# Padded small tiles, 512-column weight blocks, gate products among the decay's, and one inversion after the other in a two-layer decoder trunk

## The chip, the cores and the metric

The kernel runs on one core of one Trainium2 chip, in one launch. The metric is the device time of that launch in microseconds. A run differs from another of the same kernel by a few microseconds (2192.98 to 2197.68 here). The engines are named as in the profile: PE is TensorE (PEld its weight loads), DVE is VectorE, ACT is ScalarE, POOL is GpSimd, SP is SyncE, which issues most DMAs.

## What is computed

Two layers over 512 positions and 1024 features, in float32. Layer 0 is a half-step SwiGLU feed-forward (FFN), an RWKV-7 time mix and another half-step FFN. Its output gives one shared set of keys and values. Layer 1 is a half-step FFN, differential attention on the shared keys and values, and a last half-step FFN. Cut to what the change touches:

```python
def swiglu(h, w_in, w_out):                      # w_in 1024 x 5632, w_out 2816 x 1024
    gate, up = jnp.split(h @ w_in, 2, axis=-1)
    return (jax.nn.silu(gate) * up) @ w_out

def rwkv7_time_mix(h, mu, w_rkv, w0, w1, w2, a0, a1, a2, g1, g2, ...):
    dx = h_prev - h
    r, k, v = jnp.einsum('sbtc,scd->sbtd', h[None] + dx[None] * mu[:3, None, None, :], w_rkv)
    w_log = -jax.nn.softplus(-(w0 + jnp.tanh(xw @ w1) @ w2)) - 0.5
    decay = jnp.exp(-jnp.exp(w_log.astype(jnp.float32)))
    a = jax.nn.sigmoid(a0 + (xa @ a1) @ a2)
    g = jax.nn.sigmoid(xg @ g1) @ g2
    ...
    y = wkv7_scan(heads(r), heads(decay), heads(k), heads(v), -kk, kk * a_h)
    ...
    return (y.astype(h.dtype) * g) @ w_o

def shared_kv(x, kv_norm, w_kv, k_norm):
    kv = rms_norm(x, kv_norm) @ w_kv             # first half keys, second half values
```

## The kernel before

Activations lie with features on the 128 partitions and the 512 positions along the free axis: eight tiles `x` of 128 x 512. Every product in float32 is made of three fp32r matmuls: weight and activation are each split into a high and a low half (`whi`, `wlo`, `xgh`, `xgl`, `acth`, `actl`), and `mm3` (lines 196 to 198) adds high x high, high x low and low x high in one PSUM bank. A raw weight block `wraw` comes by DMA on SP, ACT copies it to `whi`, and DVE subtracts to `wlo`. In a row of the trace the moving operand stands first, the stationary one second.

The work goes in this order. **FFN** (four times, `ffn`): 22 pairs of gate and up features in three groups of 8, 8 and 6; in-products move `xgh` and `xgl` over `whi` and `wlo` (512 columns); out-products (`out`) move `acth` and `actl`, 12 buffers in the FFN's own pool. In the last FFN the last group is `natural`: there the act tiles are stationary, weights are moved in blocks of 256 columns (`wblock_k`, 4 rows of k to a tile), for each block the four position tiles t follow one another, and each result of 128 x 256 is added and stored at once. **Time mix** (`rwkv`): LoRA products (weights in BK, then sA), then for p of 0 to 7 a decay and an a product of 64 rows, each followed by a sigmoid on ACT (lines 650 and 652); `mixed(2)` makes the values' input (`xmt` scaled on ACT, line 636, added on DVE, line 637, then split, `xgl` on line 204); then eight gate products of four matmuls, copied by ACT to the single buffer `t0` (line 669) and stored to g_d; then `values`, four blocks of 256 columns, into four PSUM banks a block, while `recs` makes the decay's scans on DVE (line 680, tile `t1`); then the keys, where `key_done` also makes the `scores` that the inversion needs, then the receptances r. The inversion solves two groups of triangular blocks by 31 dependent steps of two DVE instructions each (lines 815 and 816): `inv0` works on x2 and x3 with the scratch tile `nr_t`, `inv1` on x0 and x1 with `nr_a`. From the seventh key on the program writes steps of `inv0` and then, by `both`, one step of each in turn. After it the results go through DRAM boxes, and the scan (`wkv`) begins with the products of line 952. **Shared KV**: keys by `heads`, values in four blocks of 256 columns, t by t, with `vN` scaled on ACT. **Attention** and the last FFN follow.

The order of the instructions on each engine isn't the order of the text: the tile framework schedules them at build time, by its own timeline and by when buffers come free. Addresses are set at build time too. `Rn` (line 279) is a tile of 4 numbers a partition in the pool `gp`, and `gk` (`trunk`, line 1366) of one in `kvp`, and pools lie one above the other. In the built program `xgh`, `xgl`, `whi`, `wlo`, `wraw` and `x` start 416 bytes past a multiple of 512 in each partition; BK, the act, g and u tiles of the first, second and last FFN, and kT and vN start at 448; act, g and u of the third FFN, which runs while `kvp` is open, start at 480.

## Time and profile before

| | |
|---|---|
| median of 3 runs | 2196.48 us (2192.98 to 2197.68) |
| the profiled execution | 2192.3 us, its span 2190.6 us |
| granted PE clock, mean of the span | 0.988 of full |
| PE busy | 2129.4 us, 97% of the span |
| DVE, ACT, POOL busy | 1193.8, 834.3 and 220.8 us (54%, 38%, 10%) |
| first, second, third, last FFN | some 16 to 375, 812 to 1198, 1296 to 1656, 1798 to 2187 us |
| time mix | some 375 to 812 us |

A row of the timeline gives an instruction's start and its length. Matmuls are pipelined, so the next begins before the last one's length is over: the distance of two starts is what one costs PE in a stream, and the length is more. A wait's row names the waiting instruction, what released it, and how long the engine stood. The granted clock is a share of full speed, where 1.00 is 2.4 GHz and 0.50 is 1.2.

### The profile page before, as it was taken

How to read it: one execution, taken by the hardware profiler on the slowest of the kernel's cores; microseconds unless marked ns; L12 is line 12 of the kernel's file. 1: busy time of each engine (PE TensorE's matmuls, PEld its weight loads, DVE VectorE, ACT ScalarE, POOL GpSimd, SP SyncE). 2: the span in 40 equal slices, each digit the busy share in tenths (PEclk: the TensorE clock that was granted, in tenths of full speed). 3: DMA queues.
4: the chain of work that ended last, by engine and by line, in shares of the span. 5: the costliest groups of instructions: out<-in, count | busy, mean ns of one | idle time of the engine just before them, and what ended most of it. 6: DMA issues, size and time to landing. Idle time of an engine off the chain costs nothing.

```text
span 2190.6 us, 27632 instructions
## 1 busy us (share of the span) xinstructions
PE 2129.4 (97%) x11007; PEld 1801.0 (82%) x11007; DVE 1193.8 (54%) x1902; ACT 834.3 (38%) x1429; POOL 220.8 (10%) x259
## 2 busy tenths in 40 slices
PE   9999999899969999999999999999999999999999
PEld 7888888687769878888888998888889678888888
DVE  6445445588847865444445535445356855444443
ACT  5223223688225544222224443222235754222222
POOL 1101000000232310100000001001010111100000
PEclk9999999999979999999999999999999999999999
DMA  7622333245587633322223232222332112222222
GB/s 264 221 93 87 115 101 119 64 141 140 125 195 188 174 113 96 96 96 96 96 91 101 78 97 96 96 96 96 96 96 78 40 39 96 97 95 96 96 92 82
DMA packets 276636, 239.90 MB, mean 110 GB/s; under 512 B 57114, under 2 KB 269244, under 8 KB 276508
## 3 DMA queue, kind: packets, MB, share of 16 engines
q1 hardware_dynamic: 275740, 236.05, 34.5%
q0 software_dynamic: 768, 2.10, 0.6%
q8 instruction: 86, 1.41, 0.3%
q14 instruction: 42, 0.34, 0.1%
HBM read 202.98 MB, written 28.84 MB: 106 GB/s over the span
## 4 chain that ended last, share of the span: by engine, by line
PE 87%; DVE 6%; ACT 3%; DMA 2%; issue 1%; POOL 0%; SPq 0%; DVEq 0%; ACTq 0%
PE ps L196 27%; PE ps L197 27%; PE ps L198 27%; DVE s L1190 1%; PE ps L994 1%; PE ps L958 1%; DMA g_d<-t 1%; PE ps L970 0%; PE ps L1189 0%; PE ps L993 0%; PE ps L952 0%; PE ps L964 0%; DMA am_d<-nsq 0%; DMA wraw<-in_rwkv_w_rkv_dram 0%; PE ps L985 0%
## 5 line engine op out<-in xcount | busy, mean ns | idle before, releaser
L196 PE MATMUL ps<-xgh,whi 128*128 128x512 f32 x1688 | 658.9, 393 | 4.0 <-ACT BK L652 1.9
L197 PE MATMUL ps<-xgl,whi 128*128 128x512 f32 x1688 | 657.5, 391 | 0.0
L198 PE MATMUL ps<-xgh,wlo 128*128 128x512 f32 x1688 | 649.8, 390 | 0.0
L161 ACT CAST whi<-wraw 128x1024 fp32r<-128x1024 f32 (+2 forms) x296 | 303.2, 1028 | 883.3 <-PE ps L197 582.9
L162 DVE TENSOR_TENSOR wlo<-wraw,whi 128x1024 fp32r<-128x1024 f32 (+2 forms) x296 | 426.7, 1445 | 93.0 <-ACT whi L161 83.9
L196 PEld LDWEIGHTS ps<-xgh,whi 128*128 128x128 f32 x1688 | 316.9, 188 | 74.6 <-ACT BK L652 3.0
L197 PEld LDWEIGHTS ps<-xgl,whi 128*128 128x128 f32 x1688 | 317.7, 188 | 66.5 <-issue 1.4
L198 PEld LDWEIGHTS ps<-xgh,wlo 128*128 128x128 f32 x1688 | 317.6, 188 | 65.8
L395 POOL TENSOR_TENSOR u<-u,g 128x512 f32<-128x512 f32 x88 | 124.3, 1413 | 1382.2 <-ACT whi L161 882.2
L196 PE MATMUL ps<-acth,whi 128*128 128x512 f32 x656 | 258.5, 395 | 0.0
L198 PE MATMUL ps<-acth,wlo 128*128 128x512 f32 x656 | 258.1, 394 | 0.0
L197 PE MATMUL ps<-actl,whi 128*128 128x512 f32 x656 | 258.0, 393 | 0.0
L394 DVE TENSOR_TENSOR u<-ps,R 128x512 f32<-128x512 f32 x88 | 60.8, 691 | 288.9 <-PE ps L198 288.9
L437 DVE SCALAR_TENSOR_TENSOR x<-ps,x 128x512 f32<-128x512 f32 x88 | 60.5, 690 | 224.1 <-PE ps L198 224.0
L196 PE MATMUL ps<-whi,xgh 128*128 128x256 f32 x512 | 145.6, 289 | 3.7 <-ACT t L669 3.5
L198 PEld LDWEIGHTS ps<-acth,wlo 128*128 128x128 f32 x656 | 123.0, 188 | 29.8
L197 PEld LDWEIGHTS ps<-actl,whi 128*128 128x128 f32 x656 | 123.0, 187 | 29.2
L197 PE MATMUL ps<-wlo,xgh 128*128 128x256 f32 x512 | 145.1, 285 | 1.8 <-DVE wlo L178 1.8
L196 PEld LDWEIGHTS ps<-acth,whi 128*128 128x128 f32 x656 | 123.1, 188 | 28.6
L198 PE MATMUL ps<-whi,xgl 128*128 128x256 f32 x512 | 144.4, 284 | 0.0
L391 DVE TENSOR_TENSOR g<-ps,R 128x512 f32<-128x512 f32 x88 | 60.8, 691 | 107.8 <-PE ps L198 107.7
L203 ACT CAST acth<-u 128x512 fp32r<-128x512 f32 x88 | 54.7, 621 | 123.9 <-POOL u L395 123.9
(330 smaller groups left out, 2404.0 us busy)
## 6 DMA issues: line engine op xcount, KB each, us to landing
wraw<-in_ffn_w_in_dram SPq DMA_DIRECT2D x87, 1024.0 KB, 5.1
wraw<-in_ffn_w_out_dram SPq DMA_DIRECT2D x32, 1024.0 KB, 5.0
boxes<-nr_a SPq DMA_DIRECT2D x64, 192.0 KB, 3.9
wraw<-in_ffn_w_out_dram SPq DMA_DIRECT2D x16, 768.0 KB, 4.3
wraw<-in_rwkv_w_rkv_dram SPq DMA_DIRECT2D x12, 1024.0 KB, 5.4
wraw<-in_w_kv_dram SPq DMA_DIRECT2D x8, 1024.0 KB, 5.3
am_d<-nsq SPq DMA_DIRECT2D x16, 256.0 KB
AM<-am_d SPq DMA_DIRECT2D x16, 256.0 KB, 4.3
```

What stands on the lines that cost most here:

```text
L161: self.nc.scalar.copy(hi[:, ks], raw[:, :, c : c + P])
L162: (eng or self.nc.vector).tensor_sub(lo[:, ks], raw[:, :, c : c + P], hi[:, ks].bitcast(F32))
L196: mm(ps, wh, xh, start=start, stop=False)
L197: mm(ps, wh, xl, start=False, stop=False)
L198: mm(ps, wl, xh, start=False, stop=stop)
L203: self.nc.scalar.copy(hi, src)
L391: nc.vector.tensor_mul(g, pg, self.R)
L394: nc.vector.tensor_mul(u, pu, self.R)
L395: nc.gpsimd.tensor_mul(u, u, g)
L437: nc.vector.scalar_tensor_tensor(x, ps, 0.5, x, ALU.mult, ALU.add)
L958: mm(p1[:, p, :], bbd[:, p, :], mv[:, p, :], start=True, stop=True)
L994: mm(py[:, p, cols], V[:, p, :], KM[:, p, cols], start=c == 0, stop=True)
```

## The change

There are four parts.

1. `Rn` becomes a tile of 128 numbers a partition of which four are used, `gk` one of 128 of which one is used. In the built program after it, every tile named above with 448 or 480 starts at 416.
2. A new generator `wrows` gives weights row by row: raw tiles of 4 rows of k x 512 columns, high and low tiles of 2 x 512. The values of the time mix, the values of the shared KV and `natural` take two blocks of 512 columns instead of four of 256. In the first block of `natural` and in both value products, k is the outer loop and t the inner one, over four PSUM banks; in `natural`'s second block t is the outer loop. Each output goes out in eight pieces of 128 x 512 rather than sixteen of 128 x 256.
3. The gate product q stands after decay product q + 3, its weights are loaded ahead of the loop, and its copy is DVE's, to `t1` with two buffers. `mixed(2)` comes after the loop, and its scaling is DVE's.
4. `both` goes. `feed` runs six steps of `inv0` at k of 2, 4 and 6, and `inv1` is run from `r_done` and after it.

```diff
+    def wrows(self, src):
+        nc = self.nc
+        kt = src.shape[0] // P
+        src = src.rearrange("(k p) f -> p k f", p=P)
+        for k in range(0, kt, 2):
+            if k % 4 == 0:
+                n = min(4, kt - k)
+                raw = self.tl(self.wp, "wraw", (P, 4, 512), bufs=2)
+                nc.sync.dma_start(raw[:, :n], src[:, k : k + n, :])
+            r = raw[:, k % 4 : k % 4 + 2]
+            hi = self.tl(self.wp, "whi", (P, 2, 512), F32R, bufs=3)
+            lo = self.tl(self.wp, "wlo", (P, 2, 512), F32R, bufs=3)
+            nc.scalar.copy(hi, r)
+            nc.vector.tensor_sub(lo, r, hi.bitcast(F32))
+            for i in range(2):
+                yield hi[:, i], lo[:, i]
...
-        rn = self.tl(self.gp, "Rn", (P, 4))
+        rn = self.tl(self.gp, "Rn", (P, P))[:, 0:4]
...
-                for b in range(0, C, 256):
-                    wb = self.wblock_k(w_out[j0 * P : j1 * P, b : b + 256])
+                for b in range(0, C, 512):
+                    wb = self.wrows(w_out[j0 * P : j1 * P, b : b + 512])
...
-                    t = self.tl(kt, "xmt", bufs=2)
-                    nc.scalar.activation(t, h[k][:, 1:], AF.Copy, scale=self.omu[:, i : i + 1])
+                    if s == 2:
+                        nc.vector.tensor_scalar_mul(t, h[k][:, 1:], self.omu[:, i : i + 1])
+                    else:
+                        nc.scalar.activation(t, h[k][:, 1:], AF.Copy, scale=self.omu[:, i : i + 1])
...
-                t = self.tl(kt, "t0")
-                nc.scalar.copy(t, ps)
-                nc.sync.dma_start(d["g"][p], t)
+            for p in range(KT + 3):
+                if p < KT:
...
+                if p >= 3:
+                    q = p - 3
+                    c = slice(q * P, (q + 1) * P)
+                    ps = self.ps()
+                    self.mm3(ps, g2h[:, c], g2l[:, c], gh, gl, True, False)
+                    mm(ps, w3[:, c], z3, start=False, stop=True)
+                    t = self.tl(kt, "t1", bufs=2)
+                    nc.vector.tensor_copy(t, ps)
+                    nc.sync.dma_start(d["g"][q], t)
+            xv = mixed(2)
...
-            def values(blocks, x, vn_of, aside):
-                for b in blocks:
-                    wb = self.wblock_k(prm["w_rkv"][2][:, b * 256 : (b + 1) * 256])
-                    pss = [self.ps()[:, :256] for _ in range(4)]
+            def values(x, vn_of, aside):
+                for b in range(2):
+                    wb = self.wrows(prm["w_rkv"][2][:, b * 512 : (b + 1) * 512])
+                    pss = [self.ps() for _ in range(4)]
+                    for k, (hi, lo) in enumerate(wb):
+                        for t in range(4):
+                            tt = slice(t * P, (t + 1) * P)
+                            self.mm3(pss[t], x[k][0][:, tt], x[k][1][:, tt], hi, lo, k == 0, k == KT - 1)
...
-            def both():
-                for _ in range(40):
-                    run(inv0, 1)
-                    yield
-                    run(inv1, 1)
-                    yield
...
+                if k in (2, 4, 6):
+                    run(inv0, 6)
...
-                run(steps, 10)
+                run(inv1, 5)
...
-            run(steps, 80)
+            run(inv1, 40)
...
-        gk = kvp.tile([P, 1], F32, tag="gk", name="gk")
+        gk = kvp.tile([P, P], F32, tag="gk", name="gk")[:, 0:1]
```

How this stands in the built order, at three places. The first is PE where the decay's products end and the gate's begin. Before (`xgh_2831` is the input of the decay and a products, `xgh_2866` that of the gate's; L667 is the gate's fourth matmul):

```order
L196 MATMUL ps_2989<-xgh_2831,whi_2910 128x512
L197 MATMUL ps_2989<-xgl_2832,whi_2910 128x512
L198 MATMUL ps_2989<-xgh_2831,wlo_2911 128x512
L196 MATMUL ps_3064<-xgh_2866,whi_3052 128x512
L197 MATMUL ps_3064<-xgl_2867,whi_3052 128x512
L198 MATMUL ps_3064<-xgh_2866,wlo_3053 128x512
L667 MATMUL ps_3064<-xgh_2900,whi_3056 128x512
L196 MATMUL ps_3072<-xgh_2866,whi_3052 128x512
L197 MATMUL ps_3072<-xgl_2867,whi_3052 128x512
```

After (L702 is that fourth matmul now):

```order
L702 MATMUL ps_2968<-xgh_2900,whi_2920 128x512
L702 MATMUL ps_2986<-xgh_2900,whi_2920 128x512
L215 MATMUL ps_2999<-xgh_2831,whi_2910 128x512
L216 MATMUL ps_2999<-xgl_2832,whi_2910 128x512
L217 MATMUL ps_2999<-xgh_2831,wlo_2911 128x512
L215 MATMUL ps_3004<-xgh_2866,whi_2916 128x512
L216 MATMUL ps_3004<-xgl_2867,whi_2916 128x512
L217 MATMUL ps_3004<-xgh_2866,wlo_2917 128x512
L702 MATMUL ps_3004<-xgh_2900,whi_2920 128x512
L215 MATMUL ps_3012<-xgh_2831,whi_2910 128x512
L216 MATMUL ps_3012<-xgl_2832,whi_2910 128x512
```

The eight gate products stood in a row behind the last decay product; now the first gate products stand among the decay's, and all eight still come before the first value product.

The second place is DVE in the same stretch. Before (L178 makes the values' `wlo`, L637 and L204 the values' input):

```order
L637 SCALAR_TENSOR_TENSOR xmt_3008<-h_396_2644,vec_534,xmt_3008 128x512
L637 SCALAR_TENSOR_TENSOR xmt_3015<-h_397_2645,vec_534,xmt_3015 128x512
L178 TENSOR_TENSOR wlo_3138<-wraw_3135,whi_3137 128x1024
L204 TENSOR_TENSOR xgl_3012<-xmt_3008,xgh_3011 128x512
L204 TENSOR_TENSOR xgl_3019<-xmt_3015,xgh_3018 128x512
L178 TENSOR_TENSOR wlo_3142<-wraw_3135,whi_3141 128x1024
L178 TENSOR_TENSOR wlo_3294<-wraw_3291,whi_3293 128x1024
L637 SCALAR_TENSOR_TENSOR xmt_3022<-h_398_2646,vec_534,xmt_3022 128x512
L637 SCALAR_TENSOR_TENSOR xmt_3029<-h_399_2647,vec_534,xmt_3029 128x512
```

After (L704 copies a gate product to `t1`, L667 scales the values' input, L670 and L223 are the old L637 and L204, L197 the old L178):

```order
L704 COPY t_477_3009<-ps_3004 128x512
L223 TENSOR_TENSOR xgl_3090<-xmt_3086,xgh_3089 128x512
L704 COPY t_481_3027<-ps_3022 128x512
L667 TENSOR_SCALAR xmt_3100<-h_398_2646,omu 128x512
L223 TENSOR_TENSOR xgl_3097<-xmt_3093,xgh_3096 128x512
L670 SCALAR_TENSOR_TENSOR xmt_3100<-h_398_2646,vec_534,xmt_3100 128x512
L667 TENSOR_SCALAR xmt_3107<-h_399_2647,omu 128x512
L704 COPY t_485_3045<-ps_3040 128x512
L197 TENSOR_TENSOR wlo_3142<-wraw_3139,whi_3141 128x1024
L704 COPY t_487_3053<-ps_3048 128x512
```

The gate's copies and the scalings are now DVE's, between the pieces of the values' input, and four of the copies stand ahead of the values' first `wlo`; the fifth is right ahead of it.

The third place is DVE in the inversion, during the r products. Before (x2, x3 and nr_t are `inv0`'s, x0, x1 and nr_a are `inv1`'s):

```order
L815 TENSOR_TENSOR nr_t_682_4218<-x2_520_3133,x3_521_3134 128x256
L815 TENSOR_TENSOR nr_a_754_4600<-x0_518_3131,x1_519_3132 128x60
L816 TENSOR_TENSOR x3_521_3134<-x3_521_3134,nr_t_682_4218 128x16x16
L816 TENSOR_TENSOR x1_519_3132<-x1_519_3132,nr_a_754_4600 128x30x2
L815 TENSOR_TENSOR nr_t_682_4218<-x2_520_3133,x3_521_3134 128x255
L815 TENSOR_TENSOR nr_a_754_4600<-x0_518_3131,x1_519_3132 128x87
```

After (L841 and L842 are the old L815 and L816):

```order
L841 TENSOR_TENSOR nr_t_674_4006<-x2_520_3133,x3_521_3134 128x256
L841 TENSOR_TENSOR nr_a_746_4427<-x0_518_3131,x1_519_3132 128x60
L842 TENSOR_TENSOR x3_521_3134<-x3_521_3134,nr_t_674_4006 128x16x16
L842 TENSOR_TENSOR x1_519_3132<-x1_519_3132,nr_a_746_4427 128x30x2
L841 TENSOR_TENSOR nr_t_674_4006<-x2_520_3133,x3_521_3134 128x255
L841 TENSOR_TENSOR nr_a_746_4427<-x0_518_3131,x1_519_3132 128x87
```

Nothing moved here: the same steps of both groups alternate at the same place, as they do from `inv1`'s first step to `inv0`'s last, and POOL's instructions keep their order in the whole program.

## Rows read from the trace of the kernel before

**Rows 1.** The page, parts 1 and 4: busy time, and the chain that ended last.
```profile
PE 2129.4 (97%) x11007; PEld 1801.0 (82%) x11007; DVE 1193.8 (54%) x1902; ACT 834.3 (38%) x1429; POOL 220.8 (10%) x259
...
PE 87%; DVE 6%; ACT 3%; DMA 2%; issue 1%; POOL 0%; SPq 0%; DVEq 0%; ACTq 0%
```

**Rows 2.** Waits of TensorE, all: us in total, times, longest.
```profile
PE ps L952 <- DMA x<-boxes: 19.6, 1, 19.6
...
PE ps L196 <- ACT t L669: 3.5, 2, 2.2
...
PE ps L196 <- ACT BK L652: 1.9, 1, 1.9
PE ps L197 <- DVE wlo L178: 1.8, 1, 1.8
```

**Rows 3.** Timeline, TensorE: start us, us, line; first and last products of runs.
```profile
121.69 0.40 PE L196 MATMUL ps<-acth,whi 128*128 128x512 f32 x1
...
166.50 0.40 PE L196 MATMUL ps<-xgh,whi 128*128 128x512 f32 x1
...
253.35 0.39 PE L198 MATMUL ps<-xgh,wlo 128*128 128x512 f32 x1
...
375.54 0.40 PE L196 MATMUL ps<-xgh,BK 128*128 128x512 f32 x1
...
386.26 0.40 PE L197 MATMUL ps<-xgl,BK 128*128 128x512 f32 x1
...
1404.49 0.40 PE L196 MATMUL ps<-acth,whi 128*128 128x512 f32 x1
...
1448.23 0.39 PE L198 MATMUL ps<-acth,wlo 128*128 128x512 f32 x1
```

**Rows 4.** The page, part 5: count, busy us, mean ns of one, idle before.
```profile
L196 PE MATMUL ps<-acth,whi 128*128 128x512 f32 x656 | 258.5, 395 | 0.0
```

**Rows 5.** Timeline, TensorE: products of 256 columns, shared KV and last block.
```profile
1214.71 0.28 PE L196 MATMUL ps<-whi,xgh 128*128 128x256 f32 x1
...
1215.91 0.28 PE L197 MATMUL ps<-wlo,xgh 128*128 128x256 f32 x1
...
2152.89 0.37 PE L196 MATMUL ps<-whi,acth 128*128 128x256 f32 x1
...
2186.93 0.28 PE L198 MATMUL ps<-whi,actl 128*128 128x256 f32 x1
```

**Rows 6.** Instructions by line and form, VectorE: count, busy us, mean ns.
```profile
L437 DVE SCALAR_TENSOR_TENSOR x<-ps,x 128x512 f32<-128x512 f32 x88 | 60.5, 690 | 224.1 <-PE ps L198 224.0
...
L1234 DVE COPY qT<-ps 128x512 f32<-128x512 f32 x8 | 5.5, 684 | 2.1 <-ACT qsq L1230 2.1
...
L1177 DVE TENSOR_SCALAR bias<-toe 128x512 f32<-128x512 f32 x8 | 3.2, 413 | 0.0
```

**Rows 7.** DMA issues: count, KB each, median us from issue to landing.
```profile
x_d<-x SPq DMA_DIRECT2D x8, 256.0 KB, 2.1
...
out_dram<-xn SPq DMA_DIRECT2D x16, 128.0 KB, 1.7
```

**Rows 8.** Timeline, TensorE: first decay product and first key product.
```profile
404.42 0.96 PE L196 MATMUL ps<-xgh,whi 64*128 64x512 f32 x5
...
478.80 0.40 PE L196 MATMUL ps<-xgh,whi 128*128 128x512 f32 x1
```

**Rows 9.** Stretches: busy us and count per engine, granted clock, DMA share, GB/s.
```profile
404.00:490.00 86.00, 78.52 (x515) 70.51 (x513) 65.01 (x87) 69.95 (x132) 0.00 (x0) 0.94 0.34 111
410.00:420.00 10.00, 8.07 (x25) 5.73 (x23) 3.51 (x6) 9.96 (x18) 0.00 (x0) 0.66 0.00 0
440.00:450.00 10.00, 10.00 (x86) 10.00 (x85) 8.84 (x12) 10.00 (x26) 0.00 (x0) 1.00 0.36 111
```

**Rows 10.** The chain of waits, 386 to 520 us: start us, us, what.
```profile
427.63 5.21 DMA g_d<-t
```

**Rows 11.** Timeline, VectorE: a step of the second group's inversion.
```profile
601.44 0.43 DVE L816 TENSOR_TENSOR x<-x,nr_a 128x255 f32<-128x255 f32 x1
```

More of the change, by code (lines that the diff above doesn't have):

```diff
@@ L635, in mixed @@
                     t = self.tl(kt, "xmt", bufs=2)
[L636 removed]
+                    if s == 2:
+                        nc.vector.tensor_scalar_mul(t, h[k][:, 1:], self.omu[:, i : i + 1])
+                    else:
+                        nc.scalar.activation(t, h[k][:, 1:], AF.Copy, scale=self.omu[:, i : i + 1])
                     nc.vector.scalar_tensor_tensor(t, h[k][:, 0:T], self.v("mu", i), t, ALU.mult, ALU.add)
@@ L643, in rwkv @@
             wh, wl = self.wflat([(prm["w2"], 0), (prm["a2"], 64)], P)
[L644 to L655 removed]
+            g2h, g2l = self.wflat([(prm["g2"][0:P], 0)], P)
             w3 = self.tl(self.wp, "whi", (P, 8, P), F32R, bufs=3).rearrange("p k f -> p (k f)")[:96]
@@ L662, in rwkv @@
             self.tl(self.wp, "wlo", (P, 8, P), F32R, bufs=3)
-            for p in range(KT):
-                c = slice(p * P, (p + 1) * P)
-                ps = self.ps()
-                self.mm3(ps, wh[:, c], wl[:, c], gh, gl, True, False)
-                mm(ps, w3[:, c], z3, start=False, stop=True)
-                t = self.tl(kt, "t0")
-                nc.scalar.copy(t, ps)
-                nc.sync.dma_start(d["g"][p], t)
+            for p in range(KT + 3):
+                if p < KT:
+                    c = slice(p * P, (p + 1) * P)
+                    for i, hh in enumerate(half):
+                        ps = self.ps()
+                        self.mm3(ps, wh[hh, c], wl[hh, c], zh[hh], zl[hh], True, True)
+                        if i == 0:
+                            nc.scalar.activation(A[:, p, :], ps, AF.Sigmoid, bias=self.v("w0", p))
+                        else:
+                            sig = nc.scalar.activation(BK[:, p, :, 0:L], ch(ps), AF.Sigmoid, bias=self.v("a0", p))
+                if p >= 3:
+                    q = p - 3
+                    c = slice(q * P, (q + 1) * P)
+                    ps = self.ps()
+                    self.mm3(ps, g2h[:, c], g2l[:, c], gh, gl, True, False)
[4 more added lines that the diff above has]
+            xv = mixed(2)
+            xvl = self.last.ins
             oka = self.tl(kt, "oka", (P, KT))
@@ L734, in recs @@
                     yield
-            xq = lambda i: X[i].rearrange("p a (t f) -> p a t f", f=256)
-            values(range(4), xv, lambda b: [xq(2 + b % 2)[:, i] for i in range(2)], recs())
+            values(xv, lambda b: X[2 * b : 2 * b + 2], recs())
             def key_cb(p, ps):
@@ L844, in rwkv @@
             xr = mixed(0)
-            def both():
-                for _ in range(40):
-                    run(inv0, 1)
-                    yield
-                    run(inv1, 1)
-                    yield
-            steps = both()
             def feed(k):
```

76 lines of the change are left out of this document (30 added, 46 removed).

## The prediction, as it was made

> **What bounds the kernel now.** I read the page's busy shares and its chain first: TensorE (PE) is busy 97% of the span and 87% of the chain that ended last is PE [rows 1]. So time is won in two ways only: fewer or shorter matmuls, and the few places where PE waits. For the first I took the distance from one matmul's start to the next, not the durations: durations overlap (0.39 us each, a new one every 0.23), starts don't. For the second I read PE's waits: one of 19.6 us in front of the scan, and 3.5, 1.9 and 1.8 us in the stretch from 404 to 490 us [rows 2], where the change moves most. That stretch I then read by tenths and by engine.
>
> **Part 1, the padded tiles.** `Rn` takes 16 bytes and `gk` 4 before, 512 each after. In the built program the tiles allocated above `Rn` start 448 bytes past a multiple of 512 (the act tiles of the first, second and last FFN, and BK), those above `gk` 480 (the third FFN's), while xgh, whi and wlo start at 416. After, all start at 416. In-products move xgh over whi, both at 416: 384 starts from 166.50 to 253.35 us, 86.85/383 = 226.8 ns [rows 3]. Out-products have the same shape and differ by the moving tile, act: at 448, 192 from 121.69 us to the next product's start at 166.50 44.81/192 = 233.4 ns; at 480, 192 from 1404.49 to 1448.23 us, 43.74/191 = 229.0 ns [rows 3]. The LoRA products, with BK at 448 as the weight and xgh moving, go from 375.54 to 386.26 us in 46 steps of 233.0 ns [rows 3]. Two unrelated tiles at 448 cost 6.4 ns a matmul and one at 480 costs 2.2, all at the full clock, so I read this as a price of the tiles' starts. Of the 656 x 3 out-products [rows 4] 528 are in each of the first three FFNs and 384 in the last: 1440 x 6.5 + 528 x 2.2 = 10.5 us, and some 120 LoRA products x 6 ns = 0.7. They run back to back on PE, so all of it is on the path: **-11.2 us**. Bounds: 0 if the offset isn't the cause, 11.2.
>
> The Trainium skill ("SBUF — State Buffer", section "Operand start alignment") asks only that an operand start at a multiple of its element size, and "TensorE: Matmul & The Clock Gate" ("Step-by-step: what each phase is for") gives PE two independent read ports, one for the streamed operand and one for the weights. By these a start of 448 is as good as 416, and this part would give nothing. The rows at 226.8, 229.0 and 233.4 ns speak against it, but no row shows one product at two starts.
>
> **Part 2, blocks of 512 instead of 256.** One product of 512 moving columns takes the place of two of 256: by the count of rows in the order that is 192 pairs in the values of the time mix, 192 in those of the shared KV and 144 in the last FFN's final block, 528 PE rows fewer. 256-column products start every 120 ns (1214.71 to 1215.91 us in ten steps) and those of the last block every 118.6 (2152.89 to 2186.93 us, 287 steps) [rows 5]. Two of them are 240 or 237, one wide one 226.8: 13 and 10 ns a pair. Shared KV 192 x 13 = 2.5 us, last block 144 x 10 = 1.5: **-4.0 us**; the values' 2.5 are counted in part 3. Weights come in chunks of 2 x 512 instead of 4 x 256, so ACT and VectorE (DVE) convert as much, and PE works 24 x 0.227 = 5.4 us on each: no new wait. Below it can't go, since the count is fixed; above, 4.0 is all.
>
> "TensorE: Matmul & The Clock Gate" in the Trainium skill (section "Back-to-back issue gap") gives N/2.4 + 2.5 ns for a warm product alone, 215.8 for 512 columns and 109.2 for 256; merging would then save 2.5 ns a pair, some 1.3 us with the values in place of 6.5. The rows, 120 and 226.8, decide for the larger.
>
> The tail gets longer: DVE's last addition goes from 128x256 to 128x512, which takes 0.69 us in the other FFNs, about 0.3 more, and the last output is 256 KB, for which x_d's row says 2.1 us where 128 KB take 1.7 [rows 6, 7]: **+0.7 us** (0.3 to 1).
>
> **Part 3, the stretch from 404 to 490 us.** Before, the decay and a products start at 404.42 us and the first key product at 478.80 [rows 8]: 74.4 us. PE's work there is 48 decay, 32 gate and 384 value products: 80 x 0.230 + 384 x 0.120 = 64.5, so 9.9 are lost: PE outruns the sigmoids on ACT (1.9 us on BK), and the gap costs it the clock too (0.66 granted from 410 to 420), then it waits on the gate's PSUM banks (3.5 us on t, because ACT's copy waits for g_d's landing to free the single t buffer, 5.2 us the longest in the chain), and 1.8 on wlo [rows 2, 9, 10]. After, the order has the gate's products between the decay's, ahead of any value product, so PE has 32 products to do while ACT's 16 sigmoids go by; the copies are on DVE, with two buffers; the values are 192 x 0.227 = 43.6. PE needs 80 x 0.227 + 43.6 = 61.8 us: the most to be won is 12.6.
>
> What is late next is DVE. Between 404 and 490 it is busy 65.0 of 86 us [rows 9]. It gets 8 copies from PSUM (0.684 by the nearest row) and 8 multiplications (0.413) [rows 6]: 8.8 us by durations, and since such rows overlap where one follows another, while the busy time counts no overlap, I take 7.7. Then 72.7 us of DVE work, in order, must be done before the first keys' last steps; with some 3 to 4 us at the start in which it has nothing, that is 76 to 77 us from 404 where it took 86: the keys' first results come about **9.5 us** earlier. I take that, with the range 0 (all of DVE's 21 idle us stay) to 12.6. ACT loses the 8 copies and 8 of its scalings, and isn't late.
>
> What waits behind the new DVE copies: each needs its PE product and a t1 buffer, which is free when g_d two copies ago has landed; behind the fifth stands the first wlo of the values, behind the eighth the decay scans, which take t1 too. With two buffers and landings up to 5.2 us [rows 10] a copy can go every 2.9 us at worst, 23 us for eight, and PE has value products from the fifth on. SP issues the values' second raw block ahead of the last two g_d; it needs only the conversion of the first.
>
> **Part 4, the inversion.** The text changes (inv0 alone at k = 2, 4, 6, then inv1), but DVE's rows of lines 815 and 816 stand in the same order in both programs, two and two alternating, and so do GpSimd's rows: the scheduler sets it. The wait of 19.6 us for boxes, which the inversion's end is behind [rows 2], stays: **0**, bounds 0 and -9 (below).
>
> **Sum.** 11.2 + 4.0 + 9.5 - 0.7 = 24.0 us off the profiled run's 2192.3 (span 2190.6): 2168.3. The median of the three runs, 2196.48, lies 4.2 above that run, so **2172** by the median.
>
> **Rivals.** (1) The starts don't matter and out-products are slower for something else, such as the engines that write act while PE reads it: part 1 falls away, 24.0 - 11.2 = 12.8, 2183 by the median. For it: no row with one product at both starts. Against: 448 gives the same price to act and to BK, 480 another. (2) DVE bounds the middle: its idle 21 us can't be used since they are waits for h, the scores and ACT, and the 7.7 us come on top: part 3 gives 0, 2182 by the median. For it: DVE at 8.8 of 10 from 440 to 450 [rows 9]. Against: those tenths are the backlog of what ACT's late copies held up. (3) The inversion does run alone. The steps of inv1 stand between inv0's, up to 0.43 us each [rows 11] and some 33 of them until inv0's end; at 0.28 from start to start they take 9 us, and the wait shrinks by that: 2163. Against: the order. (4) **Slower**: DVE's in-order waits for g_d. If landings with two 1 MB weight blocks under way take far longer than the 5.2 us seen, copies pace everything behind them. It decides once it eats the whole 24.0 us. The seven steps between eight copies, 2.9 us each at the pace above, must then take 24/7 = 3.4 us more, 6.3; two buffers make that 12.6 a landing and its copy, so landings of 12 us, over twice the longest row [rows 10]. From there it is 2197 and up; at 16 us the steps are 8.3, 38 us are lost, and it is 2211.
>
> **How the numbers follow.** Forecast 0.66, (1) 0.12, (2) 0.13, (3) 0.04, (4) 0.05. Range: the forecast's own is 2165 to 2177 (part 3 between 5 and 12.6, the tail); up to the rivals (1) and (2) it reaches 2185; below, 2163. (3) and (4) and both of (1) and (2) together stay out. This kernel can be told from no change at about 0.2%, 4.4 us. All of the forecast, (1), (2) and (3) are faster by more; with (1) and (2) together (0.02) it would be near the bound: faster 0.93, same 0.03, slower 0.04.
>
> **What would show it.** Right: out-products and LoRA products at 227 ns in all four FFNs; 512-column products at 227 in the values, the shared KV and the last block; the first key product about 64 to 66 us after the first decay product, without waits on L669's copy; the 19.6 us wait unchanged. Wrong: out-products still at 233 (rival 1); PE waits on wlo or xgl in the values, DVE without idle time from 404 on and the first keys not earlier (rival 2); a shorter wait before L952 (rival 3); DVE idle on g_d landings (rival 4).

## The result: 2168.9 us, where the 24.4 us came from

The changed kernel took 2168.89 us (median of four runs, 2167.57 to 2170.8) against 2196.78 for the kernel before on the same chip; the ratio is 0.9877, 95% interval 0.986 to 0.9894. Its profiled execution took 2167.88 us with a span of 2166.2, so the two spans differ by 24.4 us; by the medians it is 27.9, and 21.7 and 24.2 in two later sets of runs of the same program. The prediction was 24.0 off the profiled run, 2172 by the median, with 2163 to 2185 as its range. The profiled runs differ as the sum said; the median of the changed kernel lies only 1.0 us above its profiled run, and not 4.2 as in the kernel before, which is where 2172 is too high.

The page of the changed kernel, its parts 1 and 5; they answer to [rows 1, 4]:

```profile
PE 2111.3 (97%) x10479; PEld 1772.6 (82%) x10479; DVE 1199.1 (55%) x1908; ACT 822.9 (38%) x1395; POOL 221.3 (10%) x259
...
L215 PE MATMUL ps<-acth,whi 128*128 128x512 f32 x656 | 254.7, 389 | 0.0
```

PE is 18 us less busy and still 97% of its span. The out-products' mean length falls from 395 to 389 ns, which says little; the starts say it. The timeline of PE in the changed kernel, the same runs of products as in [rows 3, 8]:

```profile
121.85 0.39 PE L215 MATMUL ps<-acth,whi 128*128 128x512 f32 x1
...
165.37 0.39 PE L215 MATMUL ps<-xgh,whi 128*128 128x512 f32 x1
...
372.09 0.39 PE L215 MATMUL ps<-xgh,BK 128*128 128x512 f32 x1
...
382.74 0.40 PE L217 MATMUL ps<-xgh,BK 128*128 128x512 f32 x1
...
400.38 0.50 PE L215 MATMUL ps<-xgh,whi 64*128 64x512 f32 x2
...
462.32 0.39 PE L215 MATMUL ps<-xgh,whi 128*128 128x512 f32 x1
...
1384.07 0.39 PE L215 MATMUL ps<-acth,whi 128*128 128x512 f32 x1
...
1427.59 0.39 PE L215 MATMUL ps<-xgh,whi 128*128 128x512 f32 x1
```

Out-products of the first FFN: 192 steps from 121.85 to 165.37 us, 226.7 ns (233.4 before). LoRA products: 47 steps from 372.09 to 382.74, 226.6 ns (233.0). Third FFN: 192 steps from 1384.07 to 1427.59, 226.7 ns (229.0). In these streams the products of 512 columns now cost the same, in-products and out-products alike. The rows of 400.38 and 462.32 are the first decay product and the first key product: 61.94 us apart where it was 74.38.

Cut at the starts of such products, the two spans compare like this (us; a stretch ends where the next begins):

| stretch | before | after | change | predicted |
|---|---|---|---|---|
| start to the first decay product (first FFN, LoRA) | 404.42 | 400.38 | -4.04 | -4.1 |
| first decay product to first key product | 74.38 | 61.94 | -12.44 | } -9.5 |
| first key product to the last receptance product | 118.95 | 122.65 | +3.70 | } together |
| wait for boxes, and the scan | 191.63 | 191.49 | -0.14 | 0 |
| output projection, start of the second FFN | 66.94 | 65.50 | -1.44 | 0 |
| second FFN | 341.79 | 338.19 | -3.60 | -3.4 |
| shared keys and values, to the third FFN's first product | 97.56 | 95.12 | -2.44 | -2.5 |
| third FFN | 360.16 | 358.81 | -1.35 | -1.2 |
| attention, start of the last FFN | 185.22 | 186.26 | +1.04 | 0 |
| last FFN up to its last block | 308.19 | 305.55 | -2.64 | -2.5 |
| last block, tail | 41.36 | 40.31 | -1.05 | -0.8 |

The waits of PE in the changed kernel (us in total, times, longest) that answer to [rows 2]:

```profile
PE ps L971 <- DMA x<-boxes: 18.3, 1, 18.3
...
PE ps L773 <- ACT nacc L768: 5.0, 3, 3.2
...
PE ps L215 <- ACT BK L696: 0.6, 1, 0.6
```

The waits on the gate's copy (3.5 us) and on wlo (1.8) are gone, the one on BK fell from 1.9 to 0.6, the one for boxes is 18.3 where it was 19.6. What is new is the third wait, on nacc: 5.0 us in three times with 3.2 the longest. It was 2.9 in all before, so 2.1 of the table's +3.70 are this wait. The other 1.6 come behind it. Stretches of the changed kernel, as in [rows 9] (length; PE, PEld, DVE, ACT, POOL busy; granted clock, DMA share, GB/s):

```profile
400.00:486.00 86.00, 82.19 (x353) 63.27 (x352) 77.03 (x109) 70.29 (x122) 1.91 (x2) 0.96 0.37 123
410.00:420.00 10.00, 10.00 (x41) 6.75 (x41) 9.25 (x16) 8.41 (x14) 0.00 (x0) 0.84 0.35 131
408.38:476.53 68.15, 64.85 (x279) 51.64 (x279) 65.80 (x94) 55.22 (x100) 1.91 (x2) 0.97 0.42 139
476.00:486.00 10.00, 9.47 (x31) 6.97 (x32) 7.44 (x10) 8.94 (x13) 0.00 (x0) 0.83 0.33 105
```

DVE is busy 77.0 of 86 us where it was 65.0, and the clock between 410 and 420 us is 0.84 instead of 0.66. In the ten us behind the long wait, which ends at 476.53, the granted clock is 0.83: products of 512 columns start 427 ns apart there from 478.3 to 481.3 us, the lower level, before they are back at 0.23 us. From the end of that wait to the last receptance product it is 108.44 us, against 106.84 in the kernel before, whose wait at this place was 1.0 us: that is the 1.6. The chain of waits in the changed kernel shows what the keys wait for (start us, us, what):

```profile
464.62 7.29 DMA v_d<-x
...
472.18 0.91 DVE x L833
473.09 1.21 DVE xmt L670 x2
...
474.85 0.90 ACT whi L161
...
475.80 0.69 ACT nacc L768
...
476.53 1.13 PE ps L773 x2
```

The row of 7.29 us is a store of the values to v_d. After it DVE clears x3 for the first inversion (L833), behind that in DVE's order stand two steps of the keys' input (xmt), behind those ACT's xgh and the keys' weights, behind those the first key's nacc, and PE stands still for it until 476.53, which is 76.15 us after the first decay product. From 408.38 us to there DVE is idle for 2.4 of 68.2 us (65.80 busy, third row above), and 1.2 of these are the wait for the store in front of L833.

### The profile page after: what moved, and what is told of

The parts are those of the page before. It is cut to its first block, busy times and chain, and to the rows that moved or that the text cites. A ratio compares the mean times of both kernels' runs of the same rounds, so it can differ in the third digit from the quotient of the medians.

```text
span 2166.2 us, 26528 instructions
## 1 busy us (share of the span) xinstructions
PE 2111.3 (97%) x10479; PEld 1772.6 (82%) x10479; DVE 1199.1 (55%) x1908; ACT 822.9 (38%) x1395; POOL 221.3 (10%) x259
## 4 chain that ended last, share of the span: by engine, by line
PE 88%; DVE 6%; DMA 2%; ACT 2%; issue 1%; POOL 1%; SPq 0%; DVEq 0%; ACTq 0%
PE ps L215 27%; PE ps L216 26%; PE ps L217 26%; DVE s L1209 1%; PE ps L1013 1%; DMA boxes<-x 1%; PE ps L1012 1%; PE ps L989 0%; PE ps L977 0%; PE ps L999 0%; POOL boxes L849 0%; PE ps L1003 0%; PE ps L1208 0%; PE ps L971 0%; DMA wraw<-in_rwkv_w_rkv_dram 0%
## 5 line engine op out<-in xcount | busy, mean ns | idle before, releaser
L215 PE MATMUL ps<-whi,xgh 128*128 128x256 f32 (+1 forms) x384 | 122.8, 323 | 0.2 <-DVE mx L1209 0.2
L216 PE MATMUL ps<-wlo,xgh 128*128 128x256 f32 (+1 forms) x384 | 122.3, 319 | 0.0
L217 PE MATMUL ps<-whi,xgl 128*128 128x256 f32 (+1 forms) x384 | 122.2, 318 | 0.0
```

The lines of the kernel that those rows point to most:

```text
L215: mm(ps, wh, xh, start=start, stop=False)
L216: mm(ps, wh, xl, start=False, stop=False)
L217: mm(ps, wl, xh, start=False, stop=stop)
```

## Experiments

### The tiles' starts

**Pads alone.** The kernel before with part 1 of the change and nothing else.

```diff
-        rn = self.tl(self.gp, "Rn", (P, 4))
+        rn = self.tl(self.gp, "Rn", (P, P))[:, 0:4]
-        gk = kvp.tile([P, 1], F32, tag="gk", name="gk")
+        gk = kvp.tile([P, P], F32, tag="gk", name="gk")[:, 0:1]
```

> The kernel before with Rn and gk padded to 512 bytes and nothing else, so that act, BK and the rest start at 416 like xgh and whi. If the start of the tiles is what makes out-products and LoRA products slow: both go from 233.4 and 233.0 ns a product to 226.8, the third FFN's from 229.0 to 226.8, and the run is 11.2 us shorter, about 2185.5. If the start doesn't matter and act is slow for another reason: 233 stays and the time is that of before, 2196.8, within 2 us.

Measured: 2184.0 us against 2194.1, ratio 0.9954 (0.9936 to 0.9972), so -10.1 us, and 226.7 ns a product in all four FFNs and the LoRA products. Rival (1), by which the starts don't matter, falls. But one start was compared with another only where both the start itself and its distance from whi's changed. The next three tell these apart.

The last block, where weights of 256 columns still move over act, went the other way. Its first and its last product (timeline of PE):

```profile
2142.65 0.36 PE L196 MATMUL ps<-whi,acth 128*128 128x256 f32 x1
...
2177.17 0.28 PE L198 MATMUL ps<-whi,actl 128*128 128x256 f32 x1
```

That is 120.3 ns a product over 287 steps where the kernel before takes 118.6 [rows 5], 0.5 us in all: for 256 columns equal starts were a little slower, not faster.

**All tiles 32 bytes further.** The changed kernel with a tile more among the constants; xgh, whi, wlo, act and BK all start at 448.

```diff
+        const.tile([P, 8], F32, tag="shift", name="shift")
         self.ident = const.tile([P, P], F32, tag="ident", name="ident")
```

> The changed kernel with 32 bytes more among the constants, so that every tile of a product, moving and stationary, starts at 448. If 448 is a bad start by itself: all products of 512 columns, in-products too, at 233 ns, and some 40 us longer. If it is the distance between the starts of the two operands: 226.8 ns everywhere and 2169.

Timeline of PE in that kernel, out-products of the first FFN and the in-products after them:

```profile
121.76 0.39 PE L216 MATMUL ps<-acth,whi 128*128 128x512 f32 x1
...
165.28 0.39 PE L216 MATMUL ps<-xgh,whi 128*128 128x512 f32 x1
...
252.10 0.39 PE L218 MATMUL ps<-xgh,wlo 128*128 128x512 f32 x1
```

192 steps to 165.28 us, 226.7 ns; 383 more to 252.10, 226.7 ns. The run took 2171.1 us. So 448 is no bad start by itself: what counts is how far the starts of the moving and the stationary tile lie apart.

**A distance of 256, and of 192 the other way.** The kernel before with `Rn` of 64 numbers and `gk` of 16: act starts at 160, in the third FFN at 224, whi at 416.

```diff
-        rn = self.tl(self.gp, "Rn", (P, 4))
+        rn = self.tl(self.gp, "Rn", (P, 64))[:, 0:4]
-        gk = kvp.tile([P, 1], F32, tag="gk", name="gk")
+        gk = kvp.tile([P, 16], F32, tag="gk", name="gk")[:, 0:1]
```

> The kernel before with Rn padded to 256 bytes and gk to 64, so that act starts at 160 in the first, second and last FFN and at 224 in the third, with xgh, whi and wlo at 416: distances of 256 and 320 bytes instead of 32 and 64. If a whole 512 bytes is needed: between 229 and 234 ns or more in all FFNs. If 32-byte or 64-byte steps are what counts (a distance that is a multiple of 64 being cheap): 226.8 to 229 in all four, and 2186 to 2188.

Timeline of PE, first and next product after 192 out-products, in the first FFN and in the third:

```profile
122.30 0.39 PE L196 MATMUL ps<-acth,whi 128*128 128x512 f32 x1
...
165.82 0.39 PE L196 MATMUL ps<-xgh,whi 128*128 128x512 f32 x1
...
1404.31 0.40 PE L196 MATMUL ps<-acth,whi 128*128 128x512 f32 x1
...
1448.28 0.40 PE L196 MATMUL ps<-xgh,whi 128*128 128x512 f32 x1
```

226.7 ns in the first FFN (and in the second, the last and the LoRA products), 229.0 in the third. The third costs what 64 bytes cost before, and 160 costs nothing: a tile need not be padded to 512 bytes. The time, 2191.3, tells little: in this one run the stretch from the last receptance product to the scan's end took 7.5 us longer than in the kernel before, and that varies by itself, as the runs on the inversion show.

**A distance of 128, and of 224.** The kernel before with `Rn` of 32 numbers and `gk` of 24: act starts at 32, in the third FFN at 128.

```diff
-        rn = self.tl(self.gp, "Rn", (P, 4))
+        rn = self.tl(self.gp, "Rn", (P, 32))[:, 0:4]
-        gk = kvp.tile([P, 1], F32, tag="gk", name="gk")
+        gk = kvp.tile([P, 24], F32, tag="gk", name="gk")[:, 0:1]
```

> The kernel before with Rn padded to 128 bytes and gk to 96, so that act starts 128 bytes from whi in the first, second and last FFN, and 224 in the third. Distances of 0 and 256 gave 226.7 ns, 64 and 192 gave 229.0, 32 gave 233.3. If the price goes by the distance modulo 128: 226.7 ns at 128 and 233.3 at 224. If only multiples of 256 are free: 128 costs something between 227 and 233, and 224, near 256, may cost less than 233.

The same rows of PE's timeline:

```profile
121.34 0.40 PE L196 MATMUL ps<-acth,whi 128*128 128x512 f32 x1
...
166.13 0.39 PE L196 MATMUL ps<-xgh,whi 128*128 128x512 f32 x1
...
1407.54 0.40 PE L196 MATMUL ps<-acth,whi 128*128 128x512 f32 x1
...
1452.34 0.39 PE L196 MATMUL ps<-xgh,whi 128*128 128x512 f32 x1
```

233.3 ns in both: 192 steps from 121.34 to 166.13 us and from 1407.54 to 1452.34. The third FFN, at 229.0 before, became slower, and the run took 2197.67 us. The rule modulo 128 that I had put first falls. All the distances measured, with the moving tile's start minus the stationary one's reckoned modulo 256, are these:

| distance modulo 256 | seen as | ns a product |
|---|---|---|
| 0 | in-products; act 256 below whi; everything after the change | 226.7 |
| 64 | act 64 above whi (before), 192 below | 229.0 |
| 32 | act 32 above whi (before) | 233.3 to 233.4 |
| 128 | act 384 below whi | 233.3 |
| 224 | act 288 below whi; xgh 32 below BK (before) | 233.0 to 233.3 |

Period 256 fits every row, the two repeats among them (64 above and 192 below, 32 below and 288 below); why 64 is cheaper than 128 no run here shows. The table holds for 512 columns. The last block's products of 256 columns took 120.3 ns when whi and act started equally or 256 bytes apart (pads alone, and the kernel with 256), 118.6 at 32 bytes apart and 119.0 at 384.

### The wide blocks and the middle, each alone

**Wide blocks alone.** The kernel before with `wrows` in the values, in the shared KV and in `natural` (part 2).

```diff
-                for b in range(0, C, 256):
-                    wb = self.wblock_k(w_out[j0 * P : j1 * P, b : b + 256])
+                for b in range(0, C, 512):
+                    wb = self.wrows(w_out[j0 * P : j1 * P, b : b + 512])
...
-            for b in range(0, C, 256):
-                wb = self.wblock_k(w_kv[:, C + b : C + b + 256])
+            for b in range(0, C, 512):
+                wb = self.wrows(w_kv[:, C + b : C + b + 512])
```

> The kernel before with the 512-column weight blocks alone (values of the time mix, values of the shared KV, last block). By the price of a pair (240 against 226.8 ns, 237 against 226.8): -2.5 in the shared KV, -1.5 in the last block, +0.7 at the tail, and up to -2.5 in the values if PE bounds them: 2190.5 to 2193.5. If a product of 512 columns cost only 2.5 ns a pair less than two of 256: 2196 or above.

Measured: 2192.45 us against 2194.1, ratio 0.9993 (0.9984 to 1.0003); the median lies in the expected range, but the interval of the ratio allows no gain at all. The trace says where the parts are. The shared KV is 2.42 us shorter, as priced. In the values the first key product comes 3.1 us earlier, and by the last receptance product 1.6 are left. The last block and the tail together are only 0.1 us shorter. Its products (timeline of PE):

```profile
2152.34 0.48 PE L215 MATMUL ps<-whi,acth 128*128 128x512 f32 x1
...
2185.78 0.40 PE L217 MATMUL ps<-whi,actl 128*128 128x512 f32 x1
```

That is 233.8 ns a product over 143 steps, where they take 227.5 in the changed kernel. Here act is the stationary tile, whi moves, and the two still lie 32 bytes apart. So the parts aren't independent. Where the starts are 32 bytes apart, two products of 256 columns take 237.2 ns and one of 512 takes 233.8: 3 ns a pair. Where they agree it is 240.6 (pads alone) and 227.5: 13.

**The middle alone.** The kernel before with part 3: gate products among the decay's, their copies and the scalings on DVE; the values stay in blocks of 256.

```diff
-                nc.scalar.copy(t, ps)
-                nc.sync.dma_start(d["g"][p], t)
+            for p in range(KT + 3):
...
+                if p >= 3:
+                    q = p - 3
...
+                    t = self.tl(kt, "t1", bufs=2)
+                    nc.vector.tensor_copy(t, ps)
+                    nc.sync.dma_start(d["g"][q], t)
+            xv = mixed(2)
```

> The kernel before with the gate's products among the decay's, the gate's copies and the scalings of the values' input on DVE, and nothing else; the values stay in blocks of 256. If the waits on the gate's banks and the half clock are won back and DVE then sets the first keys: -5 to -8 us, about 2190, with the first key product 9 to 10 us earlier and a wait of 1 to 4 us in the keys. If DVE takes it all back: 2196 to 2198.

Measured: 2186.32 us against 2194.1, ratio 0.9965 (0.9954 to 0.9976), -7.8 us. First decay and first key product (timeline of PE):

```profile
405.85 0.50 PE L196 MATMUL ps<-xgh,whi 64*128 64x512 f32 x2
...
470.74 0.40 PE L196 MATMUL ps<-xgh,whi 128*128 128x512 f32 x1
```

64.89 us apart, 9.49 less than before; the keys then give 1.1 back and wait 3.5 us on nacc. At the last receptance product 8.38 us are left. With the wide blocks on top, in the changed kernel, it is 12.44 at the first key product and 8.74 at the last receptance product: the 2.5 us of the values' merged pairs reach the first key and stop there. With the middle alone the longest wait on nacc is 1.7 us, the clock behind it stays at 1.00, and from its end to the last receptance product it is 106.87 us; in the changed kernel the wait is 3.2 and the same stretch 108.44.

The three parts alone make -10.1, -1.7 and -7.8 us by the medians, 19.6 together; the program of the whole change makes 21.7 on the same chip (the next run). Of the 2.1 that are lacking, 1.4 are the last block, where the wide blocks need the pads; the rest isn't told apart here from the kernel's own variation.

### The inversion

**The old alternation put back.** The changed kernel with part 4 undone.

```diff
+            def both():
+                for _ in range(40):
+                    run(inv0, 1)
+                    yield
+                    run(inv1, 1)
+                    yield
...
-                run(inv1, 5)
+                run(steps, 10)
```

> The changed kernel with the old alternation of the two inversions in the text. Since the built order is then the same on every engine, the time is that of the changed kernel, 2168.9 within 2 us, and the wait for boxes stays 18 to 20 us. If the text of the inversion moved anything: 4 us or more slower.

Measured: 2172.43 us (2168.37 to 2173.42) against 2194.1, ratio 0.9899 (0.9879 to 0.9919). Every engine's instructions are built in the same order and on the same addresses as in the changed kernel, so this is the changed kernel's program once more, and the 3.5 us over 2168.9 can't come from the edit; the number I expected was too narrow. The wait (PE's waits):

```profile
PE ps L978 <- DMA x<-boxes: 20.5, 1, 20.5
```

It is 20.5 us in this run and 18.3 in the changed kernel's, with the same program. The changed kernel itself, run again:

> The changed kernel itself, on the chip of the other three, as what they are held against: 2167 to 2172. The part that varies from run to run is expected between the end of the receptance products and the end of the scan.

Measured: 2171.36 us (2166.95 to 2173.49) against 2195.52, ratio 0.9887 (0.9872 to 0.9903). The stretch from the last receptance product to the end of the scan took 191.5 us in the changed kernel's profile, 191.4 in this one and 197.1 with the alternation in the text; from the first decay product to there the three agree within 1.2 us. Most of what differs between these three runs lies in this stretch. It begins with the long wait, in which the granted clock falls to half, and it goes on at half until it is granted again. Two stretches after the wait in the changed kernel, and the second of them with the alternation in the text:

```profile
600.00:620.00 20.00, 14.55 (x73) 14.10 (x73) 5.41 (x16) 1.64 (x4) 7.87 (x9) 0.55 0.95 235
620.00:640.00 20.00, 17.68 (x149) 16.91 (x150) 9.43 (x24) 7.96 (x20) 5.25 (x4) 1.00 0.80 218
```

```profile
620.00:640.00 20.00, 17.41 (x128) 16.76 (x128) 6.86 (x19) 6.92 (x18) 4.80 (x4) 0.87 0.75 214
```

One program, and from 620 to 640 us the granted clock is 1.00 in the one run and 0.87 in the other. Of the 5.6 us between the two stretches the wait for boxes makes 2.2 and the time outside waits 3.8; the other waits are 0.4 shorter.

**The first group really by itself.** The changed kernel with the second group's steps queued on DVE behind the first group's end.

```diff
-                    nc.vector.tensor_mul(t3, ...)
-                    nc.vector.tensor_add(D3[:, j + 1 :, :w], D3[:, j + 1 :, :w], t3)
+                    with tc.issue_after(done0[0]) if g else ExitStack():
+                        nc.vector.tensor_mul(t3, ...)
+                        nc.vector.tensor_add(D3[:, j + 1 :, :w], D3[:, j + 1 :, :w], t3)
...
-                nc.vector.tensor_copy(M3, D.rearrange("p (i j) -> p j i", j=32))
+                turned = nc.vector.tensor_copy(M3, D.rearrange("p (i j) -> p j i", j=32))
+                if g == 0:
+                    done0.append(turned.ins)
```

> The changed kernel with the second group's steps queued on DVE behind the end of the first group's, so that the first runs by itself as the words of the change say. If the 33 steps of the second group in between hold up the first: its end comes 9 us earlier, the wait for boxes shrinks from 18.3 to 9 to 11 us, and the run is 7 to 9 us shorter, about 2161, provided that the second group, then 1 to 3 us later, is not missed. If the second group is: the gain comes back as a wait later, 2166 to 2169.

Measured: 2167.96 us (2166.97 to 2172.55) against 2194.24, ratio 0.9879 (0.9856 to 0.9903). The last step of the first group on DVE in the changed kernel and then in this one:

```profile
587.40 0.18 DVE L842 TENSOR_TENSOR x<-x,nr_t 128x31 f32<-128x31 f32 x1
```

```profile
580.60 0.19 DVE L845 TENSOR_TENSOR x<-x,nr_t 128x31 f32<-128x31 f32 x1
```

It ends 6.8 us earlier, not 9, and 0.6 of the 6.8 were there before the first decay product. Alone, a step waits for the one before it: near the end the first group's instructions, 0.45 to 0.57 us apart with one of the second group's in between, are 0.23 to 0.44 apart without it, so taking one out saves some 0.2 us and not 0.28. PE's waits in this kernel:

```profile
PE ps L976 <- DMA x<-boxes: 14.5, 2, 13.7
...
PE ps L1008 <- DMA kbd<-BK: 4.2, 2, 3.7
```

The wait for boxes is 13.7 us instead of 18.3, and 3.7 us of the gain come back in the scan, where the second unit waits for kbd from BK: in the chain that load stands behind other issues of SP. The second group's last step starts at 613.5 us instead of 600.8, and the second of the two waits on boxes, 0.8 us, is new. The number expected, 2161, was wrong because of all three; the gain that is left, 0.7 to 0.8 us of the stretch in this trace, is less than the stretch varies.

### What the keys wait for

**The halves of X swapped.** The changed kernel; the values' second block no longer goes through x3, which DVE clears next.

```diff
-            values(xv, lambda b: X[2 * b : 2 * b + 2], recs())
+            values(xv, lambda b: X[2 - 2 * b : 4 - 2 * b], recs())
```

> The changed kernel with the two halves of X swapped in the values: the first block goes through x2 and x3, the second through x0 and x1, so that the inversion's first memset, of x3, need not wait for the last store to v_d. If that wait, with the input of the keys queued behind it on DVE, makes PE stand 3.2 us before the keys' first norm: 1.5 to 3 us less than the changed kernel, about 2166.5. If DVE's work alone sets the keys: within 1 us of 2168.9.

Measured: 2166.93 us (2166.24 to 2174.4) against 2194.24, ratio 0.9878 (0.9858 to 0.9898). PE's wait on nacc:

```profile
PE ps L773 <- ACT nacc L768: 3.5, 3, 1.7
```

1.7 us at the longest instead of 3.2. DVE up to the end of that wait, and the ten us behind it (stretches as above):

```profile
407.69:474.42 66.73, 64.36 (x279) 50.55 (x279) 65.71 (x93) 55.36 (x100) 1.92 (x2) 1.00 0.43 142
474.00:484.00 10.00, 9.58 (x38) 7.24 (x39) 8.02 (x11) 9.94 (x15) 0.00 (x0) 1.00 0.31 105
```

The wait ends 74.73 us after the first decay product (76.15 and 75.56 in the changed kernel's two profiles), and the clock behind it stays at 1.00. From the first decay product to the last receptance product it is 181.59 us where the changed kernel takes 184.59 and 183.98. The same holds in all eight profiles that bear on it: 181.6 to 182.1 in the three with the swap, 184.0 to 185.1 in the five without. So clearing x3 behind the store of v_d cost some 2 to 3.5 us, about 1 of it by the later norm and 1.6 by the clock that falls in the longer wait. DVE is busy 65.7 of the 66.7 us before the norm: once the store is out of the way, it is DVE's work that sets the first keys. The medians don't show the gain: the ratio of 0.9878 is that of the changed kernel, 0.9877 to 0.9899 in its three sets of runs. In the very execution that was profiled it is hidden, since its scan stretch took 202.7 us. The second of the two stretches that were shown above, in this kernel:

```profile
620.00:640.00 20.00, 16.70 (x108) 16.28 (x107) 7.00 (x17) 6.72 (x17) 4.28 (x4) 0.74 0.77 219
```

The granted clock is 0.74 there, where it was 1.00.

**The scalings back on ACT**, with the swap.

```diff
-                    if s == 2:
-                        nc.vector.tensor_scalar_mul(t, h[k][:, 1:], self.omu[:, i : i + 1])
-                    else:
-                        nc.scalar.activation(t, h[k][:, 1:], AF.Copy, scale=self.omu[:, i : i + 1])
+                    nc.scalar.activation(t, h[k][:, 1:], AF.Copy, scale=self.omu[:, i : i + 1])
```

> The changed kernel with the halves of X swapped (as in the run before) and the eight scalings of the values' input back on ACT. If DVE sets the first keys: DVE has 3.2 us less to do, and the first keys' results come 1 to 3 us earlier than with the swap alone, PE waits less than 3.5 us on them. If ACT is as full as DVE there: the sigmoids or the conversions of the values' weights are late, and the keys come at the same time or later.

Measured: 2168.79 us (2165.68 to 2169.66) against 2195.52, ratio 0.9876 (0.9861 to 0.989). PE's wait:

```profile
PE ps L770 <- ACT nacc L765: 3.7, 3, 1.8
```

3.7 us in all against 3.5, and 181.58 us from the first decay product to the last receptance product against 181.59. It doesn't matter which of the two engines scales. That doesn't clear DVE. Up to the end of the first wait:

```profile
408.60:475.33 66.73, 64.31 (x279) 50.51 (x280) 63.75 (x88) 58.81 (x106) 1.91 (x2) 1.00 0.43 142
```

DVE is 2.0 us less busy than with the swap alone, 63.75 for 65.71, and in the same 66.73 us it stands idle 2.0 longer: from 410 to 415 us it waits 2.2 for what ACT now makes (xmt on L666 and xgh behind it). ACT is 3.5 us busier. So what DVE gained it lost by waiting for ACT, as the second case of what was expected has it; that the keys would come earlier if DVE had less to do and ACT no more, no run here shows.

**Both edits together.**

> The changed kernel with both of the last two edits: the halves of X swapped, and the second group's inversion queued behind the first's. If the two gains are of different waits, they add: 3 us in the keys (the wait before the keys' first norm) and 5 to 7 us in the wait for boxes, of which some comes back in the scan; 2162 to 2166, 4 us or more under the changed kernel on the same chip. If the scan takes it back: within 2 us of it.

Measured: 2167.44 us (2166.47 to 2168.58) against 2195.52, ratio 0.9874 (0.9857 to 0.989); the changed kernel on the same chip had 2171.36 and 0.9887. The waits:

```profile
PE ps L976 <- DMA x<-boxes: 14.9, 2, 13.9
...
PE ps L1008 <- DMA kbd<-BK: 4.1, 2, 3.4
PE ps L773 <- ACT nacc L768: 3.5, 3, 1.7
```

Both waits are smaller (nacc 3.5 for 5.0, boxes 13.9 for 18.3 and 18.6), and again some of it returns on kbd. The median is 3.9 us under the changed kernel's, but the runs overlap (2166.47 to 2168.58, 2166.95 to 2173.49) and so do the ratios' intervals. It is the kernel to build on; that it is faster is likely and not shown.

## Why the prediction was right, step by step

**The sum.** 24.0 were predicted and 24.4 measured, in part by chance: part 1 gave 0.4 us more than its term and part 3 0.8 less, the last block 0.3 more, and 0.5 came from stretches that were put at nothing.

**Part 1 was right in size, and its mechanism only in part.** 11.2 us were predicted; the FFNs and the LoRA products gave 4.04 + 3.60 + 1.35 + 2.64 = 11.6, and the pads alone 10.1 by the medians, with 0.5 lost in the last block. The prediction spoke of "a price of the tiles' starts", and held 448 and 480 against 416. It is not the start but the distance of two starts. Both readings gave the same number here, since the change made the distance zero. The page of the Trainium skill on operand starts asks for no more than the element's size ("SBUF — State Buffer", "Operand start alignment") and says that this is about legality, not speed; so it doesn't say that a start of 448 is as good as 416, as the prediction took it. Every start here was allowed. As to what it costs, 448 with 416 is 6.6 ns a product slower than 416 with 416, and the two read ports that "TensorE: Matmul & The Clock Gate" describes ("Step-by-step: what each phase is for") don't show in these rows as independent of each other.

**Part 2 was right where it was counted, and its tail was priced a little too high.** Shared KV -2.44 against -2.5. In the last block the products take 32.5 us instead of 34.0 from first to last, the -1.5 predicted; from the last product to the end it is 4.1 us instead of 3.7, +0.5 where +0.7 was put. The DMA issues in the changed kernel (count, KB, median us):

```profile
g_d<-t SPq DMA_DIRECT2D x8, 256.0 KB, 5.4
...
out_dram<-xn SPq DMA_DIRECT2D x8, 256.0 KB, 2.7
```

A 256 KB output lands in 2.7 us in the median, where the prediction took 2.1. What the prediction didn't see is that the last block's gain needs part 1: alone it was 233.8 ns a product. And the -1.5 is two things at once, 1.9 from widening at equal starts less the 0.5 by which equal starts slow the products of 256.

**Part 3 was right in its sum, 8.74 for 9.5, and in what sets the keys; it was wrong in what it drew from that for PE.** The prediction had DVE's work, in order, as what is late next: the keys' first results 76 to 77 us from the first decay product, where it had been 86. PE's first norm of the keys begins 76.15 us after it (75.56 in the second profile), where it was 86.49, and DVE is busy nearly all of the time before it. But from these first results the prediction went over to the first key product, 64 to 66 us, and that one doesn't wait for them. It came after 61.94 us, and after 60.53 in the second profile: below the 61.8 called PE's own work, since the products of 64 rows were counted one by one, where many start in pairs within 10 ns (the row of 400.38 shows two at once). So the 12.6 called the most to be won was won at that point, and PE then stood for the norm. Of the +3.70 in the keys, 2.1 are that longer wait and 1.6 the clock that fell in it; the sum had neither. Part of the wait is DVE's clearing of x3 behind the store of v_d, which the swap takes out. The prediction had looked at what waits behind the copies, not at the buffers that the new halves of X keep busy. g_d's landing, 5.4 us in the median, delayed one copy by 0.3 us: rival (4) was far off.

**Part 4 was right.** The order on the engines was the same, and the alternation in the text changed nothing. The bound of 9 us for a first group that really runs alone was too large: 6.2 on DVE, 4.6 in the wait, and 0.7 to 0.8 in the stretch.

**What was not foreseen** and cancels: -1.44 in the output projection (a wait of 1.0 us on xgh there before is gone), +1.04 in attention, where the cause is open. They are small, and one of each sign.

## What to carry to other kernels

Before tuning matmuls, take the distance of two starts in a stream for each pair of operands: products of the same shape that differ by 2 to 3% point to where the tiles lie, and padding one small tile may be worth more than a rewrite. Do so for each width that the kernel uses: here equal starts made 512 columns faster and 256 a little slower. Where a sum says when a result comes, ask which instruction waits for that result, and count as lost the clock that falls while the engine waits. Let a step into a schedule be followed by the question which buffers it keeps busy for longer, and who is queued behind the one that waits for them. And where a scheduler sets the order, compare the built orders before pricing an edit of the text: part 4 was no change at all.

## What the runs showed of the hardware

A matmul of 512 fp32r columns took 226.7 ns from start to start when the moving and the stationary tile started a multiple of 256 bytes apart, 229.0 at 64 modulo 256, and 233.0 to 233.4 at 32, 128 and 224, at the full granted clock in all of them, in the FFNs and the LoRA products (227.5 and 233.8 in the last block, at 0 and at 224); moving every tile by the same 32 bytes changed nothing. Of 256 columns it took 120.3 ns at 0, 118.6 at 224 and 119.0 at 128. A wait of 1.7 us of PE in the keys left the granted clock at 1.00 in the ten us behind it, one of 3.2 us was followed by 0.83 there and 1.6 us lost. The stretch from the last receptance product to the scan's end took between 191 and 203 us in the profiles of kernels that don't differ there, after a wait of 18 to 21 us in which the granted clock fell to 0.5; in two runs of one and the same program it was 1.00 and 0.87 from 620 to 640 us.
